# Two heads at a time in attention and retention, with a fixed matmul order, in a two-layer float32 backbone

## The chip, the cores and the metric

The kernel runs on one core of a Trainium2 chip. The metric is the device time of one execution in microseconds, from runs on that core. Its engines are TensorE (PE; PEld is its weight load), VectorE (DVE), ScalarE (ACT), GpSimd (POOL) and SyncE (SP), which here only issues DMAs. Matmuls write to PSUM, which has eight banks of 512 float32 columns on 128 partitions.

## What is computed

Two layers over 256 latent tokens and 256 context tokens of width 1024, all in float32. Each layer: a modulated RMSNorm, one input projection into three parallel groups (neighbourhood attention with 8 heads of 64, a convolution module of 256 channels and 31 taps, and bidirectional retention with 4 heads of key width 32 and value width 64), an output projection, a gated residual, then a feed-forward part: dense in layer 0, eight experts with two per token in layer 1. Layer 1 needs no context output.

```
px = ux @ w_in                       # 3072 columns: q, k, v | conv | ret q, k, v, two gates
s  = concat(q k_window + bias, q k_ctx);  p = softmax(s);  o = p v        # 8 heads of 64
y  = conv(a * sigmoid(g), 31 taps) + b;  silu(layernorm(y))
o_n = ((q_n k_n^T) * decay) v_n + (q_n * q_dec) S;   forward and backward # 4 heads, 32 x 64
y_ret = silu(g_f) * norm(o_f) + silu(g_b) * norm(o_b)
h  = h + g1 * (concat(y_na, y_conv, y_ret) @ w_out)
h  = h + g2 * (dense SwiGLU, or sum over the top 2 of 8 experts of p_e * SwiGLU_e)
```

The modulation vectors (shifts, scales, gates) are `silu(c) @ w_mod + b_mod`, 6 x 1024 for each layer.

## The kernel before

Activations are held transposed (channels on partitions, 512 tokens as columns, context first). A float32 product of full precision is made of three matmuls on a high and a low part (`three`, lines 178 to 182): `split` (lines 136 to 146) makes the high part `wh` of a weight with a ScalarE cast (line 143) and the low part `wl` with a VectorE subtraction (line 145). Plain float32 matmuls (scores, products with V, transposes) stand without the split and show as two records each in the trace.

The stages follow each other in the program: `begin` (modulation of the first norm and the convolution's projection), the mixer of layer 0, its output projection, the dense feed-forward, the mixer of layer 1, its output projection with the router, the experts.

In the mixer, `projT` and `projK` take one 1 MB chunk of `w_in` each, in halves q, and accumulate into two PSUM tiles `mm`. A string of letters gives the order in which the steps are written (`ORDER`): for layer 0 convolution (c), retention's q, k, v (r), gates (g), the first half of attention's q, k, v (p), heads 0 and 1 (0), retention's state (S) and its latent block (B), the second half (q), the switch (m) after which every attention or retention step also issues one chunk of the remaining modulation (`self.st`), convolution taps (t), heads 2 and 3 (1), retention's context block (b) and the rest. That is the order of the text. What each engine executes is decided by a scheduler, which moves instructions of all engines by its own estimate of when they are ready; only the experts have a fixed order (`manual_schedule` for PE, DVE and ACT).

Attention (`attn_lat`, from line 550) takes one head after the other: for each of two query tiles the score (line 562) into a `dn` tile, bias and row minimum on VectorE (565), the exponential (566), the reciprocal (567), the scaling (568), four transposes (571), a ScalarE copy (572), and after both tiles four products with V (575) on the 64 columns of the head in a `po` tile. `attn_ctx` (lines 578 to 604) does the same for the context. Retention (`ret_block`, from line 691) makes its decay table `Dm` anew for each head and block (612, 613), the scores on 32 rows (707), four VectorE products, and four matmuls per head on 64 columns (717 to 720); then squares, row sums (725), a power on GpSimd (728), a copy (730), transposes (733) and the gating.

A chunk of modulation (`mod_chunk`) is a 1 MB load into a `raw` tile and four matmuls on 32 columns each (line 229); 16 such chunks are made in the attention of layer 0. The `raw` pool has two buffers, which the weights of the mixer of layer 0 use as well.

In the experts, each pair of experts has its tokens gathered (`gather_x`): four steps, one per block of another expert, each for two of the eight channel tiles (the halves r). A half is four matmuls (1075) into half of one `tp` tile, a ScalarE copy with bias (1078) and a VectorE difference (1079).

PSUM: `mm` 3 banks, `dn` 2, `tp` 2, `po` 1, for the whole program.

## Time and profile before

| | |
|---|---|
| median of 3 runs | 1965.64 us (1965.2 to 1968.17) |
| profiled execution | 1965.71 us, span 1963.9 us |
| TensorE busy | 1870.9 us, 95% |
| VectorE busy | 1493.4 us, 76% |
| ScalarE busy | 1051.4 us, 54% |
| HBM read | 479.24 MB, mean 245 GB/s |

Stages by the time axis of the trace, from the span's start: `begin` to 63.84, projections of layer 0 to 142.48, its attention and retention (with the later projections) to 309.16, output projection to 356, feed-forward to 742, projections of layer 1 from 756 to 817.56, its attention and retention to 913.41, output projection and router to 957, experts to the end. A row of the timeline has start, length, engine, line, operation, tiles, shapes and the number of records merged; what stands in brackets is the idle time before it and what ended it. Records of matmuls on TensorE overlap by their modelled ends, so that a row's length is a little more than its distance to the next.

### The profile page before, as it was taken

How to read it: one execution, taken by the hardware profiler on the slowest of the kernel's cores; microseconds unless marked ns; L12 is line 12 of the kernel's file. 1: busy time of each engine (PE TensorE's matmuls, PEld its weight loads, DVE VectorE, ACT ScalarE, POOL GpSimd, SP SyncE). 2: the span in 40 equal slices, each digit the busy share in tenths (PEclk: the TensorE clock that was granted, in tenths of full speed). 3: DMA queues.
4: the chain of work that ended last, by engine and by line, in shares of the span. 5: the costliest groups of instructions: out<-in, count | busy, mean ns of one | idle time of the engine just before them, and what ended most of it. 6: DMA issues, size and time to landing. Idle time of an engine off the chain costs nothing.

```text
span 1963.9 us, 24506 instructions
## 1 busy us (share of the span) xinstructions
PE 1870.9 (95%) x9198; PEld 1474.9 (75%) x9198; DVE 1493.4 (76%) x2006; ACT 1051.4 (54%) x1371; POOL 108.0 (6%) x99
## 2 busy tenths in 40 slices
PE   5999999999999999999899999999999999999996
PEld 2886648878878789876777777887777877778774
DVE  4875354786545448846699988999899898999997
ACT  3323333332222234335588667677777777767774
POOL 2100011111111011010000000000000000000000
PEclk9999999999999999999899999999999999999998
DMA  8320355465444213315599988999999999999991
GB/s 306 110 90 30 118 209 197 169 235 193 170 156 167 86 43 129 119 53 215 193 388 359 343 333 314 365 360 344 360 354 358 354 351 352 354 359 364 345 402 68
DMA packets 71806, 481.97 MB, mean 245 GB/s; under 512 B 8320, under 2 KB 12544, under 8 KB 14464
## 3 DMA queue, kind: packets, MB, share of 16 engines
q1 hardware_dynamic: 71680, 480.32, 65.4%
q8 instruction: 76, 1.25, 0.3%
q14 instruction: 50, 0.41, 0.1%
HBM read 479.24 MB, written 1.05 MB: 245 GB/s over the span
## 4 chain that ended last, share of the span: by engine, by line
issue 53%; PE 42%; DVE 2%; POOL 1%; ACT 1%; DMA 0%; POOLq 0%; SPq 0%; DVEq 0%; ACTq 0%
PE mm L181 9%; PE mm L180 9%; PE mm L182 9%; PE dn L180 2%; PE dn L182 2%; PE dn L181 2%; PE po L575 1%; PE dn L562 1%; PE mm L229 1%; PE tp L571 1%; PE dn L707 1%; DVE wl L145 1%; POOL rms L728 1%; PE dn L586 0%; PE tp L725 0%
## 5 line engine op out<-in xcount | busy, mean ns | idle before, releaser
L145 DVE TENSOR_TENSOR wl<-rawx,wh 128x1024 fp32r<-128x1024 f32 x496 | 581.8, 1220 | 61.1 <-ACT wh L143 60.1
L143 ACT CAST wh<-rawx 128x1024 fp32r<-128x1024 f32 x496 | 490.2, 1050 | 162.9 <-PE mm L181 92.6
L180 PE MATMUL mm<-wh,xh 128*128 128x512 f32 x896 | 361.6, 404 | 4.0
L182 PE MATMUL mm<-wh,xl 128*128 128x512 f32 x896 | 354.6, 396 | 0.0
L181 PE MATMUL mm<-wl,xh 128*128 128x512 f32 x896 | 354.0, 395 | 0.0
L143 ACT CAST wh<-raw 128x1024 fp32r<-128x1024 f32 x220 | 222.3, 1051 | 202.6 <-PE mm L181 107.2
L145 DVE TENSOR_TENSOR wl<-raw,wh 128x1024 fp32r<-128x1024 f32 x220 | 262.6, 1222 | 51.9 <-ACT wh L143 50.8
L180 PE MATMUL mm<-uh,wh 128*128 128x512 f32 (+1 forms) x664 | 244.5, 371 | 5.2 <-ACT uh L418 4.2
L181 PE MATMUL mm<-ul,wh 128*128 128x512 f32 (+1 forms) x664 | 244.9, 371 | 0.9 <-DVE ul L419 0.4
L182 PE MATMUL mm<-uh,wl 128*128 128x512 f32 (+1 forms) x664 | 243.9, 369 | 0.0
L180 PEld LDWEIGHTS mm<-wh,xh 128*128 128x128 f32 x896 | 168.8, 188 | 49.5 <-ACT wh L143 12.2
L182 PEld LDWEIGHTS mm<-wh,xl 128*128 128x128 f32 x896 | 168.6, 188 | 40.4
L181 PEld LDWEIGHTS mm<-wl,xh 128*128 128x128 f32 x896 | 169.1, 189 | 34.8
L1139 PE MATMUL dn<-wh,hx 128*128 128x512 f32 x448 | 178.2, 398 | 7.5 <-DVE hx L1124 7.5
L1140 PE MATMUL dn<-wl,hx 128*128 128x512 f32 x448 | 177.3, 396 | 0.0
L180 PEld LDWEIGHTS mm<-uh,wh 128*128 128x128 f32 x664 | 125.2, 190 | 34.0 <-ACT uh L418 5.6
L181 PEld LDWEIGHTS mm<-ul,wh 128*128 128x128 f32 x664 | 125.7, 190 | 25.8 <-POOL ul L419 1.9
L182 PEld LDWEIGHTS mm<-uh,wl 128*128 128x128 f32 x664 | 125.9, 190 | 22.0 <-issue 1.1
L1121 ACT CAST hx<-tp 128x512 fp32r<-128x512 f32 x56 | 33.0, 589 | 140.5 <-PE tp L1114 140.5
L1139 PEld LDWEIGHTS dn<-wh,hx 128*128 128x128 f32 x448 | 84.4, 188 | 30.7 <-DVE hx L1124 11.4
L1140 PEld LDWEIGHTS dn<-wl,hx 128*128 128x128 f32 x448 | 84.2, 188 | 20.6
L145 DVE TENSOR_TENSOR wl<-hT,wh 128x1024 fp32r<-128x1024 f32 x70 | 83.3, 1218 | 4.3 <-ACT wh L143 4.3
(294 smaller groups left out, 2617.7 us busy)
## 6 DMA issues: line engine op xcount, KB each, us to landing
rawx<-w_moe SPq DMA_DIRECT2D x148, 1024.0 KB, 6.7
rawx<-w_moed SPq DMA_DIRECT2D x72, 1024.0 KB, 6.7
raw<-w_moe SPq DMA_DIRECT2D x54, 1024.0 KB, 6.7
raw<-w_mod SPq DMA_DIRECT2D x29, 1024.0 KB, 4.8
rawx<-w_mod SPq DMA_DIRECT2D x19, 1024.0 KB, 5.2
raw<-w_moed SPq DMA_DIRECT2D x19, 1024.0 KB, 6.3
hT<-w_moed SPq DMA_DIRECT2D x18, 1024.0 KB, 6.7
hT<-w_moe SPq DMA_DIRECT2D x17, 1024.0 KB, 6.9
```

The costliest lines, as they stand in the source:

```text
L143: nc.scalar.copy(h, r)
L145: nc.vector.tensor_tensor(l, r, h.bitcast(F32), OP.subtract)
L180: mm(ps, ah, bh, start=first, stop=False)
L181: mm(ps, ah, bl, start=False, stop=False)
L182: mm(ps, al, bh, start=False, stop=last)
L229: nc.tensor.matmul(ps[32 * j:32 * j + 32, :], self.cT[:, k, :], w[:, j, :], start=start, stop=stop)
L562: nc.tensor.matmul(sc, self.qT[r0:r0 + 64, hp, q0 + qt * P:q0 + (qt + 1) * P], self.kT[r0:r0 + 64, hp, :], start=True, stop=True)
L571: nc.tensor.transpose(tp[:, kt * P:(kt + 1) * P], p[:, kt * P:(kt + 1) * P], self.ident)
L575: nc.tensor.matmul(po[r0:r0 + 64, 0:256], self.vt[:, kt, h * 64:h * 64 + 64], pt[:, kt, :], start=kt == 0, stop=kt == 3)
L1121: nc.scalar.copy(hx[:, 0], t3)
L1139: mm(pd[n], hh[:, k], wh[:, 0, c], start=b == 0 and k == 0, stop=False)
L1140: mm(pd[n], hh[:, k], wl[:, 0, c], start=False, stop=b == NB - 1 and k == 3)
```

## The change

- Attention: `lat_unit` and `ctx_unit` take both heads of a pair at once. The two scores go into the two banks of one tile (`pair`), next to each other in the order; the products with V alternate between the two heads.
- Retention: the scores of two heads alternate into two `mm` tiles; the products alternate between two heads in one `md` tile. Decay tables are made once for each layer and head (`decays`) in the gate step.
- `attention` and `retention` are generators, a unit's score ahead of the previous unit's transposes and the unit before's output. `weave` mixes them by their numbers of steps, and `core` runs the mix under `manual_schedule` for TensorE alone: 25 and 20 steps in layer 0, 17 and 12 in layer 1.
- Convolution taps, three at a time, and the modulation chunks of layer 0 become a background (`self.bg`), of which `projT` and `projK` take one step ahead of each group of twelve or 24 matmuls. All projections now stand before `core`.
- `core` takes bias, transposed p and retention's products from three `uu` tiles.
- PSUM has two layouts (`banks`): in the mixers a pair of 2 banks, `mm` 2, `md` 1, `tp` 2, `po` 1; in feed-forward and experts as before.
- `gather_x`: the matmuls of both halves first, then the copies of both; in the steps among the experts into `po` instead of `tp`.

The core of the diff:

```diff
+    def pair(self):
+        t = self.psx.tile([P, 2, 512], F32, name="mmp", tag="mmp")
+        return [t[:, 0], t[:, 1]]
...
-        pss = [self.mm() for _ in range(2)]
+        pss = [self.mm(), self.mm()]
...
                     a, e = cut or (los[m], NTOK)
+                    next(self.bg, None)
...
+        for hh in heads:
+            r = slice(64 * hh, 64 * hh + 64)
+            nc.tensor.matmul(scs[hh], self.qT[r, hp, q0 + qt * P:q0 + (qt + 1) * P], self.kT[r, hp, :], start=True, stop=True)
...
+        def out():
+            po = self.po()
             for kt in range(4):
+                for hh in heads:
+                    h = 2 * hp + hh
+                    nc.tensor.matmul(po[64 * hh:64 * hh + 64, 0:256], self.vt[:, kt, h * 64:h * 64 + 64], pts[hh][:, kt, :], start=kt == 0, stop=kt == 3)
...
+    def attention(self, l, yt):
+        turn = out = None
+        for hp in range(4):
+            pts = []
+            for qt in (0, 1, 2)[:3 if l == 0 else 2]:
+                unit = self.lat_unit(l, hp, qt, yt, pts) if qt < 2 else self.ctx_unit(hp, yt)
+                yield
+                if out:
+                    out()
+                if turn:
+                    turn[0]()
+                    yield
+                out = turn[1] if turn else None
+                turn = unit
...
+            for n, (lo, hi, t) in enumerate(((0, 256, 0), (128, 256, 1), (256, 512, 1), (256, 384, 0))):
+                for pr in range(2):
+                    h = 2 * c + pr
+                    nc.tensor.matmul(od[64 * pr:64 * pr + 64, lo:hi], self.rv[:, g * 2 + t, h * 64:h * 64 + 64], parts[pr][n],
+                                     start=state is None and n == 0, stop=n == 3)
...
+        with self.tc.manual_schedule(engines={mybir.EngineType.PE}):
+            n = (25, 20) if l == 0 else (17, 12)
+            for _ in self.weave((n[0], self.attention(l, yt)), (n[1], self.retention(l, yt))):
+                pass
...
-    ORDER = ("crgp0SBqmt1b23M", "kcrgp0SBqt123")
+    ORDER = ("cxrgpqtA", "kcxrgpqtA")
...
+                    "x": lambda: setattr(self, "bg", self.weave((21, V["taps"]), (17, V["mods"])) if l == 0 else V["taps"]),
...
-            ps = self.dn() if first and q % 2 else self.tp()
-            for r in range(2):
-                c = slice(r * 256, r * 256 + 256)
+            ps = (self.dn() if q % 2 else self.tp()) if first else self.po()
+            cs = [slice(r * 256, r * 256 + 256) for r in range(2)]
+            for r, c in enumerate(cs):
                 k = 2 * q + r
                 for j, ut in enumerate((self.uth, self.utl)):
                     for t in range(2):
                         nc.tensor.matmul(ps[:, c], ut[:, t, k * P:(k + 1) * P], Gr[:, t, :], start=j + t == 0, stop=j + t == 2)
+            for r, c in enumerate(cs):
+                k = 2 * q + r
```

TensorE in the attention of layer 0, about its middle, before: a row is line, operation, tiles written and read, shape and count; L229 is modulation, L562 and L586 are scores, L575 products with V, L571 and L598 transposes.

```order
L229 MATMUL mm<-raw,cTp 32x512 x3
L586 MATMUL dn<-kT,qT 128x256 x3
L575 MATMUL po<-pT,vt 64x256 x4
L571 MATMUL tp<-cst,p 128x128 x4
L229 MATMUL mm<-raw,cTp 32x512
```

The same place in the changed kernel, in its fixed order: L572 and L608 are scores, L763 retention's scores, L636 products with V of the context, L588 transposes, L781 retention's products, L788 its row sums and L797 the transposes after them.

```order
L797 MATMUL mm<-cst,rmb 128x128 x4
L572 MATMUL mmp<-kT,qT 128x512 x2
L763 MATMUL mm<-mix 128x256 x4
L636 MATMUL po<-bx,vt 64x256 x4
L588 MATMUL tp<-cst,p 128x128 x8
L608 MATMUL mmp<-kT,qT 128x256 x4
L781 MATMUL md<-rx,rsd 64x256 x2
L781 MATMUL md<-rx,rsd 64x128 x2
```

The single-head groups of four and the modulation between them are gone; scores and products stand in pairs of heads, with eight transposes in a row.

SyncE's issues from the end of `begin` through the projections of layer 0, before: `raw<-w_in` is a projection's weight chunk, `raw<-w_mod` a modulation chunk, `bias<-nab` the attention bias.

```order
L133 DMA raw<-w_in 128x2048 x2
L781 DMA tab<-tab 128x1536
L560 DMA bias_413<-nab 128x256
L560 DMA bias_414<-nab 128x256
L133 DMA raw<-w_in 128x2048 x8
```

The same stretch of the changed kernel:

```order
L148 DMA raw<-w_in 128x2048
L242 DMA raw<-w_mod 128x2048
L663 DMA tab<-tab 128x1536
L568 DMA bias_415<-nab 128x256
L568 DMA bias_416<-nab 128x256
L242 DMA raw<-w_mod 128x2048
L148 DMA raw<-w_in 128x2048
L242 DMA raw<-w_mod 128x2048 x2
```

Between two weight chunks now stand one or two modulation chunks, in the same two buffers; this goes on until the last of the 16.

## Rows read from the trace of the kernel before

**Rows 1.** The page: span, and busy time of each engine.

```profile
span 1963.9 us, 24506 instructions
PE 1870.9 (95%) x9198; PEld 1474.9 (75%) x9198; DVE 1493.4 (76%) x2006; ACT 1051.4 (54%) x1371; POOL 108.0 (6%) x99
```

**Rows 2.** Stages: stretch, length, busy and records by engine, granted clock, DMA.

```profile
core 0: us, PE busy (x) PEld busy (x) DVE busy (x) ACT busy (x) POOL busy (x), PEclk, DMA share, GB/s
...
63.84:142.48 78.64, 78.64 (x433) 67.95 (x431) 67.38 (x96) 19.64 (x24) 0.00 (x0) 1.00 0.27 95
142.48:309.16 166.68, 158.47 (x771) 88.38 (x771) 76.40 (x206) 60.45 (x136) 13.25 (x9) 1.00 0.35 124
...
817.56:913.41 95.85, 90.90 (x474) 60.20 (x473) 51.54 (x133) 39.74 (x84) 7.68 (x9) 1.00 0.21 70
...
956.63:1963.90 1007.27, 963.89 (x4331) 772.26 (x4330) 919.52 (x987) 725.29 (x832) 0.73 (x1) 0.99 0.89 337
```

**Rows 3.** Groups on TensorE, 142.48 to 309.16: count | busy us, mean ns | idle before.

```profile
L229 PE MATMUL mm<-raw,cTp 128*32 128x512 f32 x128 | 28.5, 605 | 0.0
L562 PE MATMUL dn<-kT,qT 64*128 64x512 f32 x32 | 17.4, 634 | 0.0
L575 PE MATMUL po<-pT,vt 128*64 128x256 f32 x64 | 15.5, 385 | 0.0
...
L586 PE MATMUL dn<-kT,qT 64*128 64x256 f32 x32 | 9.4, 415 | 0.0
L707 PE MATMUL dn<-mix 32*128 32x256 f32 x32 | 9.4, 413 | 0.0
...
L603 PE MATMUL po<-pTc,vt 128*64 128x256 f32 x28 | 7.5, 392 | 0.0
...
L717 PE MATMUL po<-af,rsd 128*64 128x256 f32 x16 | 5.1, 403 | 0.3 <-DVE af L710 0.3
...
L718 PE MATMUL po<-af,rsd 128*64 128x128 f32 x16 | 3.2, 279 | 0.0
```

**Rows 4.** The same view of layer 1's attention, 817.56 to 913.41.

```profile
L562 PE MATMUL dn<-kT,qT 64*128 64x512 f32 x32 | 16.2, 634 | 0.5 <-DVE st L565 0.5
L575 PE MATMUL po<-pT,vt 128*64 128x256 f32 x64 | 15.5, 385 | 0.2 <-ACT pT L572 0.2
```

**Rows 5.** Single rows of TensorE's timeline in layer 0's attention: start, length.

```profile
183.57 0.38 PE L719 MATMUL po<-ab,rsd 128*64 128x256 f32 x1
183.58 0.43 PE L717 MATMUL po<-af,rsd 128*64 128x256 f32 x1
...
220.80 1.12 PE L562 MATMUL dn<-kT,qT 64*128 64x512 f32 x2
...
222.34 0.60 PE L571 MATMUL tp<-cst,p 128*128 128x128 f32 x4
...
226.47 1.13 PE L586 MATMUL dn<-kT,qT 64*128 64x256 f32 x6
227.53 1.94 PE L575 MATMUL po<-pT,vt 128*64 128x256 f32 x8
...
276.03 1.06 PE L229 MATMUL mm<-raw,cTp 128*32 128x512 f32 x8
```

**Rows 6.** The page's DMA issues: count, size each, median us to landing.

```profile
raw<-w_mod SPq DMA_DIRECT2D x29, 1024.0 KB, 4.8
```

**Rows 7.** The power on GpSimd (group, layer 0), and a wait behind it (layer 1).

```profile
L728 POOL TENSOR_TENSOR rms<-rms,cst 128x8 f32<-128x8 f32 x4 | 6.8, 1690 | 155.2 <-DVE rms L727 155.2
...
859.80 0.63 PE L733 MATMUL tp<-cst,rmb 128*128 128x128 f32 x4 [1.57 <-DVE rmb L730]
```

**Rows 8.** Waits of the gather: total, times, longest; and one of them.

```profile
PE tp L1075 <- DVE xl L1079: 14.3, 12, 1.6
...
1140.76 0.51 PE L1075 MATMUL tp<-Gr,uth 128*128 128x256 f32 x2 [1.08 <-DVE xl L1079]
```

**Rows 9.** A long idle gap of TensorE, and the stretch with the lower clock after it.

```profile
33.04 0.50 PE L180 MATMUL mm<-uh,wh 128*128 128x512 f32 x1 [4.17 <-ACT uh L418]
...
33.84:37.25 3.41, 3.29 (x8) 2.29 (x9) 2.68 (x5) 2.00 (x3) 1.88 (x2) 0.50 0.57 229
```

More of the change, by code (lines that the diff above doesn't have):

```diff
@@ L288, in mod_sums, with mod_all @@
             yield
-    def mod_all(self, l, groups, hold):
+    def mod_all(self, l, groups):
         for g in groups:
-            yield from self.mod_steps(l, g, hold)
+            yield from self.mod_steps(l, g)
     def mcol(self, l, ct, v):
@@ L452, in projK @@
         uh, ul = u
-        pss = [self.mm() for _ in range(2)]
+        pss = [self.mm(), self.mm()]
         first = [True, True]
@@ L459, in projK @@
                 c = slice((t % 2) * 256, (t % 2) * 256 + 256)
+                if t % 2:
+                    next(self.bg, None)
                 for k in range(4):
@@ L587, in attn_ctx, with ctx_unit @@
+        return turn, out if qt else None
+    def ctx_unit(self, hp, yt):
+        nc = self.nc
+        heads = (0, 1)
+        scs, ps, pts = self.pair(), [], []
+        for qt in range(2):
+            for hh in heads:
+                r = slice(64 * hh, 64 * hh + 64)
+                nc.tensor.matmul(scs[hh][:, qt * 256:qt * 256 + 256], self.qT[r, hp, qt * P:(qt + 1) * P], self.kT[r, hp, 0:256], start=True, stop=True)
+        for hh in heads:
+            sc = scs[hh]
             st = self.sm.tile([P, 6], F32, name="stc", tag="stc", bufs=4)
@@ L601, in attn_ctx, with turn @@
-            self.st()
-            for kt in range(2):
-                nc.tensor.matmul(po[r0:r0 + 64, 0:256], self.vt[:, kt, h * 64:h * 64 + 64], pt[:, kt, :], start=kt == 0, stop=kt == 1)
-        nc.vector.tensor_copy(yt[0][:, hp, 0:256], po[:, 0:256])
-    def decay(self, l, h):
+            ps.append(p)
+        def turn():
+            for hh in heads:
+                tp = self.tp()
+                for kt in range(2):
+                    for qt in range(2):
+                        nc.tensor.transpose(tp[:, kt * 256 + qt * P:kt * 256 + (qt + 1) * P], ps[hh][:, qt * 256 + kt * P:qt * 256 + (kt + 1) * P], self.ident)
+                pt = next(self.turned).rearrange("p (k q) -> p k q", k=2)
+                nc.scalar.copy(pt, tp.rearrange("p (k q) -> p k q", k=2))
+                pts.append(pt)
@@ L607, in decay, with decays @@
+    def decays(self, l):
+        self.nc.sync.dma_start(self.tab, self.A["tab"])
+        self.Dm = self.mx.tile([P, 4, 2, 256], F32, name="Dm")
+        for h in range(4):
+            self.decay(l, h, self.Dm[:, h])
+    def decay(self, l, h, Dm):
         nc = self.nc
-        Dm = self.mx.tile([P, 2, 256], F32, name="Dm", tag="p", bufs=4)
         for d in range(2):
@@ L737, in ret_block, with retention, weave, core @@
             nc.vector.tensor_tensor(yt[1][:, 2 + c, y0:y0 + 256], r[:, 0:256], r[:, 256:512], OP.add)
+            yield
+    def retention(self, l, yt):
+        self.rope()
+        yield
+        yield from self.ret_state(l)
+        yield from self.ret_block(l, 1, yt, True)
+        if l == 0:
+            yield from self.ret_block(l, 0, yt, None)
+    def weave(self, *streams):
+        done = [0] * len(streams)
+        live = list(range(len(streams)))
+        while live:
+            i = min(live, key=lambda i: (done[i] + 0.5) / streams[i][0])
+            done[i] += 1
+            if next(streams[i][1], self) is self:
+                live.remove(i)
+            else:
+                yield
+    def core(self, l, yt):
+        nc = self.nc
+        x = self.u8(name="bx")
+        for i in range(2):
+            nc.gpsimd.memset(x[:, i, 0:256], 0.0)
+        self.bias = cycle(self.bias + [x[:, i] for i in range(2)])
+        y, z = self.u8(name="rx"), self.u8(name="px")
+        self.turned = cycle([x[:, i] for i in (2, 3)])
+        self.pT = [z[:, 2 * i:2 * i + 2].rearrange("p a (k q) -> p (a k) q", k=2) for i in range(2)]
+        self.spare = cycle([y[:, i] for i in range(4)])
+        with self.tc.manual_schedule(engines={mybir.EngineType.PE}):
+            n = (25, 20) if l == 0 else (17, 12)
+            for _ in self.weave((n[0], self.attention(l, yt)), (n[1], self.retention(l, yt))):
+                pass
     MID = 4
     WCYC = 3
+    TAPS = 3
     CUTS = ((0, 256), (256, 512))
-    ORDER = ("crgp0SBqmt1b23M", "kcrgp0SBqt123")
+    ORDER = ("cxrgpqtA", "kcxrgpqtA")
     def mixer(self, l, u=None, pss=None):
@@ L1213, in run @@
             tps, hx = [], []
-            at = {0: [silu], 2: jobs[0:1], 4: jobs[1:2], 6: [lambda: next(gather, None)] if b else []}
+            at = [(0, silu), *zip((2, 4), jobs), (6, lambda: b and next(gather, None))]
             pu = self.wblock(X[e], at)
@@ L1271, in build @@
             return
+        self.banks(False)
         self.ffn()
+        self.banks(True)
         self.make_A(1, 0)
```

190 lines of the change are left out of this document (92 added, 98 removed).

## The prediction

> **What bounds the kernel now.** I read the page first, then a table by stage, then the matmul groups of one stage, then single rows. The page [rows 1] gives TensorE 95% busy against 76% for VectorE and 54% for ScalarE, so I look for TensorE work and for stretches where it waits. By stage [rows 2]: the projections (63.84 to 142.48 in layer 0) are solid TensorE. The attention stages, where one would expect waiting on softmax, are nearly solid too: 158.47 of 166.68 us busy in layer 0, 90.90 of 95.85 in layer 1, while VectorE does 76.40 and 51.54. The scheduler fills every softmax wait with projection matmuls, modulation chunks and retention. So the mixer is bound by TensorE's own work, and a change pays there only by making that work shorter, not by hiding waits. The experts (956.63 to 1963.90) have TensorE at 963.89 of 1007.27, VectorE at 919.52 and the DMA engines at 0.89: TensorE first, VectorE close behind.
>
> The work can be made shorter because part of it fills half the array. Scores take 64 rows of it (32 for retention), the products with V 64 columns. Alone, a 512-column score of two records takes 1.12 [rows 5], and eight records of 256 columns for one head take 1.94, about 0.234 a record from start to start. But where two heads happen to stand next to each other the records run together: 183.57 and 183.58 start two different heads' matmuls 0.01 apart; six score records at 226.47 are over when the next row starts 1.06 later, where six at 0.234 would take 1.40; and a modulation chunk (four matmuls on four column strips) takes 1.06 for eight records, as long as one matmul alone.
>
> **The change, part by part.** The profiled execution took 1965.71, 0.07 from the median 1965.64; its span is 1963.9, and I sum against 1965.7.
>
> *Pairs in layer 0.* The rows of [rows 3] that become pairs are L562, L575, L586, L603, L707, L717 and L718, with L719 and L720 of the same shapes and counts as the last two: 17.4 + 15.5 + 9.4 + 7.5 + 9.4 + 2 x (5.1 + 3.2) = 75.8 busy, half of it 37.9. Busy times lap over their neighbours; counted by pace it is 192 records of 256 columns at 0.234, 32 of 512 at 0.53 and 32 of 128 at 0.11, together 65.5, half 32.7. Some already run paired, so I take **-30** (20 to 37).
>
> *Pairs in layer 1.* L562 and L575 again, 16.2 + 15.5 [rows 4], and half of layer 0's retention, 13.0: half is 22, by pace 20. I take **-18.5** (12 to 22).
>
> *Modulation.* L229 has 28.5 busy for 16 chunks [rows 3]; unsplit they cost 16 x 1.06 = 17.0 [rows 5]. Before, the scheduler breaks chunks into one matmul and three, which costs two turns instead of one. In the new order all but one of the 16 stand as four together. **-10**.
>
> *Waits that vanish.* The idle of the two attention stages, 8.2 + 4.9 [rows 2]: **-13**.
>
> *Waits that come.* The woven core has a fixed TensorE order and none of the 512-column projections as filler. I walked the printed order of layer 0 by hand with the durations of [rows 5]. Work alone: scores 8 x 1.12 + 4 x 1.06, turns 24 x 0.60, products 4 x 1.94 + 4 x 1.0, retention about 5 a block (x4) and 4 for rope and state, some 64 us. The head of the core waits for rope and the first softmax, about 6; three of the four retention blocks have only one short group between the row sums (L725 before) and the transposes that need them, while the power on GpSimd alone takes 1.69 [rows 7]. Before, this same wait showed as 1.57 on TensorE; I count 1.5 x 3. The tail, the last context heads, about 3. **+14** in layer 0 (core about 77 us). Layer 1 has two blocks and no context heads, 9 + 16 x 0.60 + 8 + 10 + 4 = 41 of work: **+11** (core about 52).
>
> *The ring of two buffers.* In layer 0 the modulation loads now share two `raw` buffers with w_in, and each load waits in SyncE's order behind the one before. A load lands 4.8 after its issue [rows 6]; a chunk of projections takes 78.64 / 7 = 11.2. In total 26 loads x 4.8 / 2 = 62 us against some 135: hidden on average. But a weight load that can start only when the modulation chunk in the middle of its predecessor is consumed has about 5.6 + 1 us until it is needed, less 4.8, and then has to be converted. Below: 0, as before the change. Above: some 1.7 on each of ten chunks, 17. The order leaves the matmuls just about enough time, so I take **+5**. Conversions and bias loads queue behind a late load, but both are earlier than needed. The convolution taps are on VectorE in the projections before as well (67.38 of 78.64 busy), so their move costs nothing; if they delay evacuations it is in the next term.
>
> *Two accumulation buffers instead of three.* Every projection now waits for the evacuation of the previous one with the same buffer; with 512 columns 2.8 us lie between, with 256 columns 1.4. I take **+3** for layer 1 and **+3** for both output projections (0 to 12 together).
>
> *Decay tables* are made once per layer, on ScalarE and VectorE inside the projections: nothing on TensorE.
>
> *Gather.* Before, the second half's matmuls wait until VectorE has read the first half from the same PSUM tile: 12 waits, 14.3 us [rows 8], for example 1.08 before 1140.76. The new order issues both halves first, into `po`, which is free at that point of the block. The experts are TensorE-bound, so up to 14.3 comes back; VectorE's own waits for the copies shrink with it, but it is 91% busy. I take **-13** (0 to 14).
>
> Sum: -30 - 18.5 - 10 - 13 + 14 + 11 + 5 + 6 - 13 = -48.5; 1965.7 - 48.5 = **1917**.
>
> **The rivals.** (a) *The softmax chain becomes the bound.* With TensorE's part halved, a unit of two heads still needs its two reductions, exponentials and scalings before it can be turned. VectorE's share of the layer 0 core is about 57 of its 76.40 (the rest is splits, convolution and halved decay work) beside 64 for TensorE. If units don't overlap, 12 units and 8 units at about 8 us give 96 + 64 = 160 instead of 77 + 52: +31, **1948**. For it: both loads are near each other, and orders on VectorE are fixed where it waits for GpSimd. Against it: one unit's turn and the previous unit's output lie between a score and its turn. The Trainium skill's page TensorEngine Tiling (Array Packing), section Performance Considerations (PSUM Bottleneck), speaks for this rival: it says that tiling speeds up TensorE but not the evacuation of PSUM, which may become the bottleneck. By that rule this rival's time would hold; no row here shows a core without filler.
>
> (b) *The gather's gain stays hidden* behind VectorE's 91%: **1930**.
>
> (c) *The pairs don't run side by side* when issued in this order, so that the change doesn't do what it says: 30 + 18.5 come back, **1965.5**, no change. Against it stand the rows that show overlap between heads.
>
> (d) *The clock falls in the core; slower.* After 4.17 us without a matmul the granted clock stood at 0.50, 1.2 instead of 2.4 GHz, from 33.84 to 37.25 [rows 9]; in the attention stages, with hardly an idle gap, it is 1.00 [rows 2]. The woven cores have more gaps. The price is that the core's 64 + 41 = 105 us of matmuls take twice as long: if all of it runs at the lower level, 1917 + 105 = **2022**. It decides the sign once more than 48.5 / 105 = 46% of this work runs slow. Against it: my gaps are 1 to 2 us, and the 1.57 before 859.80 [rows 7] left layer 1's attention at 1.00 [rows 2]. The Trainium skill's page TensorE: Matmul & The Clock Gate, section "A second HAM failure mode: psum-queue depth-cycling", says that short idle times between groups of matmuls can be enough for the clock to go back and forth. By that rule this rival would happen; the trace before agrees only for the long gap.
>
> **How the numbers follow.** Forecast as summed 0.68; (a) 0.15; (b) 0.08; (c) 0.03; (d) 0.06. The forecast's own bounds are about 1898 (all pairs at their halves, no ring stall) to 1937. The range goes from 1893 to 1953, which takes in (a) and (b) and leaves out (c), (d) and little more. A measurement of this kernel can tell about 0.2%, 4 us. Faster: 0.68 + 0.15 + 0.08 = 0.91; same 0.03; slower 0.06.
>
> **What would show it.** In the changed profile: four score records of 512 columns in about 1.1 us and eight products in about 1; layer 0's first output projection near 281 instead of 309, its core near 77 us, layer 1's near 52; modulation rows of four matmuls, 1.06 each, between projection rows without waits on DMA; no wait of the gather's second half, and experts shorter by about 13. Wrong would be: projections of layer 0 beyond 145 us (the ring), cores over 95 and 70 us with TensorE waiting for VectorE (rival a), records in single file (c), a granted clock under 1.00 in the cores (d), or a gather whose saving turns up as waits on converted weights (b).

## The result, and the profile of the changed kernel

The changed kernel takes 1918.36 us (median of 4 runs), the kernel before 1966.51 beside it: ratio 0.976, interval 0.974 to 0.978. The prediction was 1917.0. The profiled execution took 1918.13, its span is 1916.3, against 1965.71 and 1963.9 before. First the page, for [rows 1]:

```profile
span 1916.3 us, 24478 instructions
PE 1821.2 (95%) x9198; PEld 1452.0 (76%) x9198; DVE 1490.4 (78%) x1998; ACT 1042.7 (54%) x1363; POOL 108.4 (6%) x103
```

The stages, for [rows 2]: stretch, length, busy time and count of TensorE, its weight loads, VectorE, ScalarE and GpSimd, granted clock, DMA share, GB/s. The rows are layer 0's projections, its core, its output projection; layer 1's projections and core; routing and experts.

```profile
core 0: us, PE busy (x) PEld busy (x) DVE busy (x) ACT busy (x) POOL busy (x), PEclk, DMA share, GB/s
62.55:201.86 139.31, 137.97 (x785) 103.15 (x783) 83.65 (x123) 31.73 (x43) 1.91 (x3) 1.00 0.56 198
201.86:280.15 78.29, 63.61 (x425) 39.54 (x424) 57.00 (x172) 40.78 (x105) 10.56 (x8) 0.96 0.16 53
280.15:327.66 47.51, 46.75 (x382) 46.00 (x383) 19.69 (x26) 13.60 (x23) 11.63 (x13) 1.00 0.33 122
...
715.00:825.81 110.81, 106.63 (x789) 101.06 (x788) 80.87 (x160) 43.73 (x72) 2.41 (x5) 0.98 0.30 102
825.81:874.43 48.62, 42.10 (x258) 25.30 (x258) 36.28 (x106) 25.08 (x60) 6.86 (x8) 0.93 0.23 74
...
911.64:1916.30 1004.66, 970.33 (x4356) 774.34 (x4356) 923.70 (x1012) 726.16 (x836) 0.96 (x2) 0.99 0.89 339
```

The two mixers have changed their shape: projections are solid, and the cores (attention and retention together), nearly solid before, now have waits: 78.29 - 63.61 = 14.7 us in layer 0. From the first projection to the output projection layer 0 takes 217.6 instead of 245.3.

The same TensorE groups as [rows 3], in layer 0's core, with the modulation group of the projections as last row (line, tiles, count | busy us, mean ns | idle before):

```profile
L572 PE MATMUL mmp<-kT,qT 64*128 64x512 f32 x32 | 9.7, 687 | 5.6 <-ACT p L615 3.5 <-DVE st L576 2.0
L596 PE MATMUL po<-px,vt 128*64 128x256 f32 x64 | 9.0, 429 | 0.0
L781 PE MATMUL md<-rx,rsd 128*64 128x256 f32 (+1 forms) x64 | 6.8, 335 | 0.1
L636 PE MATMUL po<-bx,vt 128*64 128x256 f32 x32 | 5.0, 393 | 0.1
L763 PE MATMUL mm<-mix 32*128 32x256 f32 x32 | 4.6, 400 | 0.0
L608 PE MATMUL mmp<-kT,qT 64*128 64x256 f32 x32 | 4.5, 402 | 0.0
...
L244 PE MATMUL md<-raw,cTp 128*32 128x512 f32 x128 | 18.1, 605 | 0.5 <-DMA raw<-w_mod 0.5
```

Counts are as before (four of L603's records lay just behind the stretch of [rows 3]), and a record is about as long as before, but busy time is half: the attention and retention groups 75.8 before, 9.7 + 9.0 + 6.8 + 5.0 + 4.6 + 4.5 = 39.6 now; modulation 28.5 before, 18.1 now. What TensorE waits for in that core (line waited for: us in total, times, longest):

```profile
PE mm L797 <- DVE rmb L793: 4.6, 3, 2.1
PE mmp L572 <- ACT p L615: 3.5, 3, 1.6
PE mmp L572 <- DVE st L576: 2.0, 1, 2.0
PE tp L742 <- ACT px L589: 1.2, 1, 1.2
PE mm L788 <- ACT rsq L784: 0.9, 2, 0.6
PE tp L588 <- ACT px L589: 0.7, 1, 0.7
```

And this is new: the granted clock in three stretches of the cores, in the columns of the stages (the 13th word is the clock):

```profile
206.41:209.82 3.41, 2.98 (x10) 1.14 (x6) 3.41 (x10) 0.97 (x3) 0.00 (x0) 0.50 0.29 81
271.26:274.67 3.41, 3.41 (x16) 2.05 (x18) 3.28 (x9) 1.02 (x4) 0.00 (x0) 0.50 1.00 423
831.04:837.87 6.83, 6.15 (x19) 3.32 (x18) 5.88 (x20) 3.44 (x9) 0.00 (x0) 0.50 0.20 57
```

In them TensorE runs at 1.2 instead of 2.4 GHz (two scores of one pair take 2.08 at 834.60, 1.13 elsewhere), so I count half of its busy time there as lost, an estimate: (2.98 + 3.41) / 2 = 3.2 us in layer 0, 6.15 / 2 = 3.1 in layer 1. The first and the third follow a wait of 2.04 in the head of the core, the second the longest of the waits before L797, 2.1. The timeline shows the first of these waits (start, length, engine, line, [idle before <- what ended it]):

```profile
203.59 1.23 DVE L160 TENSOR_TENSOR wl<-raw,wh 128x1024 fp32r<-128x1024 f32 x1 [3.08 <-ACT wh L158]
204.73 0.68 DVE L576 CUSTOM_DVE_ANT_0 p<-mmp,bias 128x512 f32<-128x512 f32 x1
...
205.34 0.69 DVE L576 CUSTOM_DVE_ANT_0 p<-mmp,bias 128x512 f32<-128x512 f32 x1
...
206.09 1.82 PE L572 MATMUL mmp<-kT,qT 64*128 64x512 f32 x4 [2.04 <-DVE st L576]
```

The scores were there about 203.0, but VectorE had the split of an output weight ahead of the first maximum in its order, and that split itself waited for ScalarE. The second score, 1.13 elsewhere, takes 1.82.

### The profile page after: what moved, and what is told of

Same layout as the page of the kernel before. It is cut to its first block, busy times and chain, and to the rows that moved or that the text cites. A ratio compares the mean times of both kernels' runs of the same rounds, so it can differ in the third digit from the quotient of the medians.

```text
span 1916.3 us, 24478 instructions
## 1 busy us (share of the span) xinstructions
PE 1821.2 (95%) x9198; PEld 1452.0 (76%) x9198; DVE 1490.4 (78%) x1998; ACT 1042.7 (54%) x1363; POOL 108.4 (6%) x103
## 4 chain that ended last, share of the span: by engine, by line
issue 53%; PE 27%; DVE 3%; ACT 1%; POOL 1%; POOLq 0%; DVEq 0%; ACTq 0%
PE mm L195 6%; PE mm L196 6%; PE mm L197 6%; PE dn L195 2%; PE dn L197 2%; PE dn L196 2%; DVE wl L160 1%; DVE mix L511 1%; PE po L596 1%; PE mmp L572 0%; PE tp L588 0%; ACT wh L158 0%; ACT uh L437 0%; POOL ms L402 0%; PE tp L289 0%
## 5 line engine op out<-in xcount | busy, mean ns | idle before, releaser
L160 DVE TENSOR_TENSOR wl<-rawx,wh 128x1024 fp32r<-128x1024 f32 x496 | 581.5, 1220 | 66.1 <-ACT wh L158 64.9
L197 PE MATMUL mm<-uh,wl 128*128 128x512 f32 (+1 forms) x656 | 239.5, 367 | 0.0
L195 PEld LDWEIGHTS mm<-wh,xh 128*128 128x128 f32 x896 | 168.7, 188 | 49.5 <-ACT wh L158 7.8
L1233 PEld LDWEIGHTS dn<-wh,hx 128*128 128x128 f32 x448 | 84.3, 188 | 33.7 <-DVE hx L1218 15.5
```

The lines of the kernel that those rows point to most:

```text
L160: nc.vector.tensor_tensor(l, r, h.bitcast(F32), OP.subtract)
L195: mm(ps, ah, bh, start=first, stop=False)
L197: mm(ps, al, bh, start=False, stop=last)
L1233: mm(pd[n], hh[:, k], wh[:, 0, c], start=b == 0 and k == 0, stop=False)
```

## Experiments

Every experiment starts from the changed kernel. Since most concern the cores, here is one table of their profiles: length from the first score to the first low half of the output projection (`mm<-yl`); TensorE's busy time in it; how much of that is loss at half clock (half of the busy time in the stretches at 0.50, as above); and the rest of the length, its waits. Work at full clock (busy less loss), loss and waits add up to the length by the way they are counted. All in us.

| kernel | total | ratio to before (interval) | layer 0's core: length, busy, loss, waits | layer 1's core: length, busy, loss, waits |
|---|---|---|---|---|
| changed | 1918.4 | 0.9762 (0.9741-0.9783) | 78.3, 63.6, 3.2, 14.7 | 45.6, 39.1, 3.1, 6.5 |
| gather_halves | 1930.0 | 0.9823 (0.9810-0.9837) | 79.4, 64.9, 4.3, 14.5 | 44.5, 37.6, 1.5, 6.9 |
| heads_apart | 1927.6 | 0.9815 (0.9800-0.9830) | 83.6, 70.1, 4.4, 13.5 | 46.7, 40.9, 1.4, 5.9 |
| heads_far | 1933.2 | 0.9838 (0.9823-0.9853) | 82.3, 72.6, 3.2, 9.7 | 49.5, 43.9, 3.1, 5.6 |
| core_scheduled | 1919.0 | 0.9759 (0.9745-0.9772) | 78.5, 69.5, 6.5, 9.0 | 47.0, 43.1, 3.4, 3.9 |
| state_early | 1917.5 | 0.9757 (0.9744-0.9771) | 80.6, 65.4, 7.9, 15.2 | 38.3, 33.9, 1.7, 4.5 |
| head_filled | 1919.5 | 0.9763 (0.9750-0.9777) | 78.9, 65.3, 2.9, 13.6 | 44.0, 38.3, 0, 5.8 |
| rms_later | 1927.7 | 0.9800 (0.9787-0.9813) | 86.5, 71.9, 9.3, 14.6 | 47.0, 40.1, 3.4, 6.9 |
| ctx_copied | 1918.7 | 0.9760 (0.9746-0.9773) | 80.5, 68.7, 9.1, 11.8 | 44.0, 36.5, 0, 7.5 |
| l1_early_tail | 1913.7 | 0.9732 (0.9719-0.9745) | 79.7, 65.2, 5.1, 14.5 | 37.0, 32.5, 0, 4.5 |
| no_scaling | - | - | 72.6, 59.5, 0, 13.1 | 44.9, 38.9, 3.1, 6.0 |
| filled | 1908.1 | 0.9704 (0.9690-0.9718) | 74.1, 67.7, 0, 6.4 | 37.0, 32.5, 0, 4.5 |
| filled_only | 1918.8 | 0.9753 (0.9739-0.9768) | 75.6, 68.4, 0, 7.2 | 44.0, 39.5, 0, 4.5 |

A caution on totals: the opening, which no edit touches, ended (first projection) at 31.8 us in the changed kernel's profile and between 32.7 and 35.4 in the others, so totals can't tell apart 2 or 3 us; stage lengths can.

A caution on the loss too: it differs between profiles of the same instructions. Layer 1's core is not edited in gather_halves and ctx_copied, and yet its loss is 3.1 in the changed kernel, 1.5 and 0 in these two, its length 45.6, 44.5 and 44.0. So with one profile for each kernel, 3 us of loss or 1.6 of length there are not yet the work of an edit. They also show that only half of the loss reached the length: of 3.1 us of it 1.6 did, and with less loss the waits were longer (6.5, 6.9, 7.5). Layer 0's core, unedited in gather_halves, lost 3.2 and 4.3 and took 78.3 and 79.4.

**gather_halves: the gather undone.**

```
-            ps = (self.dn() if q % 2 else self.tp()) if first else self.po()
+            ps = self.dn() if first and q % 2 else self.tp()
...
                         nc.tensor.matmul(ps[:, c], ut[:, t, k * P:(k + 1) * P], Gr[:, t, :], start=j + t == 0, stop=j + t == 2)
-            for r, c in enumerate(cs):
-                k = 2 * q + r
                 b = self.mcol(1, 24 + k, 0)
```

> The changed kernel with one part undone: each half of a gather step is scaled by ScalarE and VectorE before the second half's matmuls are issued, in the PSUM tile used before. Theory (the 12 waits of 1.1 to 1.25 us were TensorE's own path): they come back, 10 to 13 us slower than the changed kernel, 1928 to 1931. Rival (the gain is a side effect of something else in the experts, or is hidden behind VectorE): within 4 us of 1918. Third case, neither: about 1923, half of the waits was covered by converted weights coming late.

Measured 1930.02, 11.7 more. The stretch from the routing on, 1004.66 in the changed kernel, is 9.7 longer:

```profile
913.54:1927.90 1014.36, 969.34 (x4356) 777.57 (x4356) 924.27 (x1012) 726.95 (x836) 0.97 (x2) 0.99 0.89 336
```

The gather's matmuls in the experts, of the changed kernel and then of this one (count, ns, first and last start; below it, idle time of TensorE before them, or who waited for them):

```profile
L1167 PE MATMUL po<-Gr,uth x48: 277/281/287, 1081.1 to 1631.4; 128*128 128x256 f32 x48
its engine sat idle before it (us, times) until:
who waited for it (us, times):
  ACT xh L1172: 22.3, 12
```

```profile
L1167 PE MATMUL tp<-Gr,uth x48: 277/281/392, 1083.3 to 1644.5; 128*128 128x256 f32 x48
its engine sat idle before it (us, times) until:
  DVE xl L1171: 14.3, 12
```

The 12 waits of [rows 8] are back with their 14.3 us, and of these 9.7 lie in the length of the experts; the other 2 us of the total are in stretches that the edit does not touch (1.4 of them in the opening). The theory holds, but VectorE, 92% busy, took a part of the gain back. Without the 12 waits TensorE waits longer for the experts' SwiGLU products (`sg`) on VectorE; this wait in the changed kernel, then in this one (total, times, longest):

```profile
PE tp L1208 <- DVE sg L1311: 4.4, 15, 0.9
...
PE tp L1206 <- DVE sg L1309: 1.9, 3, 0.9
```

**heads_apart, heads_far: without pairs.** In the first the heads of a unit follow each other (the first diff, and the same exchange in the context units and the retention); in the second `out(hh)` issues one head's products with V, and other work lies between the two.

```
-            for kt in range(4):
-                for hh in heads:
+            for hh in heads:
+                for kt in range(4):
```
```
+                if out:
+                    out(0)
                 unit = self.lat_unit(l, hp, qt, yt, pts) if qt < 2 else self.ctx_unit(hp, yt)
                 yield
                 if out:
-                    out()
+                    out(1)
```

> The changed kernel with the same units, buffers and weave, but within a unit the products with V, the context scores and all retention scores and products are issued for one head and then for the other; only the pair of 512-column scores stays side by side. By the changed kernel's rows single file adds 1.85 to each of 8 L596 groups, 0.75 to each of 4 L608, 0.8 to each of 4 L636, 0.75 to each of 6 L763 and 1.3 to each of 6 L781: 33 us of TensorE work. Theory (running side by side is what makes the cores short): the cores' busy time rises by about 33, the waits of 21 us shrink by some 8, so 20 to 30 us slower than the changed kernel, 1938 to 1948. Rival (the fixed order and the weave carry the gain, pairs do not matter): within 6 us of 1918.

> The changed kernel with the products with V taken apart for good: head 0's are issued ahead of the next unit's scores, head 1's behind them, so that the two heads of a unit have 4 or more other matmuls between them (in the run before, where the heads only followed each other, half of the records still ran together: 16 records of L596 took 2.86 against 1.90 side by side and 3.74 at the pace of one). Retention and scores stay as in the changed kernel. Theory (side by side is worth TensorE time, and about 0.8 of such time ends up in the total, as 9.4 of 11.9 did there): 8 L596 groups at +1.85 and 4 L636 at +0.8 make 18 us of work, 10 to 18 us slower than the changed kernel, 1928 to 1936. Rival (the cores are bound by the chains of VectorE and ScalarE, so this work falls into waits of 15 and 6.5 us): within 5 us of 1918.

heads_apart cost 9.2, not 20 to 30: my price was wrong, since issuing one head after the other does not put them in single file. At full clock only L596 and L781 of the six groups grew, and by half of what single file would cost; 8 records of two heads (L608, L636) run at full clock as fast as interleaved. The two groups in layer 0's core of heads_apart, then the products of heads_far, for 9.0 and 5.0 above:

```profile
L596 PE MATMUL po<-px,vt 128*64 128x256 f32 x64 | 11.4, 385 | 0.0
...
L781 PE MATMUL md<-rx,rsd 128*64 128x256 f32 (+1 forms) x64 | 8.9, 332 | 0.0
```
```profile
L597 PE MATMUL po<-px,vt 128*64 128x256 f32 x64 | 17.0, 413 | 0.4 <-ACT px L589 0.4
...
L640 PE MATMUL po<-bx,vt 128*64 128x256 f32 x32 | 7.6, 391 | 0.6 <-DVE yt L600 0.6
```

With work between them the products take 17.0 (one group of eight ran at half clock, 3.54 instead of 1.94), so they are as long again as the 15.5 before the change, and the total rises by 14.9, as expected. In the profile it is 13.8, of which 11.2 lie in the two cores and in the stretch behind the second, where its last products stand. So the products with V owe their gain to standing side by side. For the scores and the retention no run took the heads as far apart; that pairs carry their gain is read from the groups above, which halved at equal counts. Not all of the added time arrives in layer 0: there busy time at full clock rose by (72.6 - 3.2) - (63.6 - 3.2) = 9.0, waits fell by 5.0, and the core grew by 4.0.

**core_scheduled: the order not fixed.**

```
-        with self.tc.manual_schedule(engines={mybir.EngineType.PE}):
+        if True:
```

> The changed kernel with TensorE's order in the two cores left to the scheduler instead of fixed by the weave. In the printed order the pairs mostly stay, retention scores move up into the head of the core, and some groups are cut in two. Theory (the waits of the core come from its chains; the fixed order is worth little by itself): within 5 us of 1918, with the head's waits of 2.04, 0.68 and 1.23 partly filled. Rival (the fixed order is what keeps the pairs and the waits small): 8 to 20 us slower, 1926 to 1938.

Measured 1919.0, the same. The scheduler's order waits 5.7 less in layer 0 (9.0), but cuts pairs (2.5 us more work at full clock) and has 3.3 more of loss at half clock. The fixed order by itself brings nothing that the total shows.

**state_early: less work in the head.**

```
     def retention(self, l, yt):
-        self.rope()
-        yield
-        yield from self.ret_state(l)
...
-    ORDER = ("cxrgpqtA", "kcxrgpqtA")
+    ORDER = ("cxrgSpqtA", "kcxrgSpqtA")
...
+                    "S": lambda: self.early_state(l),
```

> The changed kernel with rope and retention state of each layer moved from the head of the core into the projections, before the last two query and key projections, so that the core's weave starts with retention scores. Theory (the head's waits, 2.04 + 0.68 + 1.23 in layer 0 and 2.04 + 0.68 + 0.35 in layer 1, and the stretch at half clock that follows each are due to too little TensorE work there): waits of the head shrink to about 2 per layer, the clock stays at 1.00 there, core about 70 and 43; 6 to 10 us faster than the changed kernel, 1908 to 1912. Rival (the softmax chain of VectorE and ScalarE sets the pace of the core; work taken out of it turns into waits): within 3 us of 1918. Rival two (VectorE is full in the projections, the five rope and state operations there delay evacuations): slower than 1921.

Measured 1917.5, the same: the first rival by its number, but not by its mechanism. In layer 1 the core became 7.3 us shorter, the stretch behind it 1.5 longer. In layer 0 2.9 us less work (65.4 - 7.9 against 63.6 - 3.2) met equal waits and 4.7 us more loss at half clock, in stretches after waits in the middle of the core; the moved work made the projections before it 2.3 longer.

**head_filled, rms_later, ctx_copied: one wait each.** In this order:

```
         self.rope()
+        ps = self.tp()
+        for i in range(2):
+            self.nc.tensor.matmul(ps, self.ident, self.kT[:, i, :], start=True, stop=True)
```
```
             yield
+            yield
             rb = self.mm()
...
-            n = (25, 20) if l == 0 else (17, 12)
+            n = (25, 24) if l == 0 else (17, 14)
```
```
-            nc.vector.tensor_reduce(st[:, 0:2], sc.rearrange("p (q k) -> p q k", q=2), AX.X, OP.max, negate=True)
...
-                nc.scalar.activation(p[:, qt * 256:qt * 256 + 256], sc[:, qt * 256:qt * 256 + 256], AF.Exp, bias=st[:, qt:qt + 1], accum_out=st[:, 2 + qt:3 + qt])
+                nc.vector.tensor_tensor_reduce(p[:, qt * 256:qt * 256 + 256], sc[:, qt * 256:qt * 256 + 256], self.zeros, -1.0, 3e38, OP.add, OP.min, st[:, qt:qt + 1])
+            for qt in range(2):
+                nc.scalar.activation(p[:, qt * 256:qt * 256 + 256], p[:, qt * 256:qt * 256 + 256], AF.Exp, bias=st[:, qt:qt + 1], scale=-1.0, accum_out=st[:, 2 + qt:3 + qt])
```

> The changed kernel with two matmuls of 512 columns (2.1 us, result unused) in each core's head, behind the rope matmuls, where TensorE waits 2.04 us for the first maximum; nothing waits for them. Theory (that wait is what lets the granted clock fall to 0.50 from 206.4 to 209.8 and from 831.0 to 837.8, and rows there take twice as long, by their rows about 1.5 and 3.2 us): the wait is filled, the clock stays at 1.00 in both heads, the cores are 1 to 1.5 and 2 to 3 us shorter, 1913 to 1916. Rival (the clock falls later instead or the rows' extra time lies in waits for VectorE and ScalarE): cores as long as before within 0.5 us, 1916 to 1920.

> The changed kernel with one step more of attention between the row sums of a retention block (L788) and the transposes of their power (L797). Theory (each wait of the core is its own link of VectorE and GpSimd, and goes when more TensorE work lies in it): the waits of 1.37, 1.10 and 2.12 before L797 in layer 0 and of 1.73 in layer 1 go, and the stretch at half clock from 271.3 with them: 5 to 7 us faster than the changed kernel, 1911 to 1913. Rival (the chain through VectorE and ScalarE sets the pace): the waits move to the softmax of the context heads (L572 behind L615), within 2.5 us of 1918.

> The changed kernel with the context heads' scores read once by VectorE, which writes them to SBUF with their maximum, so that ScalarE's exponentials no longer hold the PSUM pair. Theory (TensorE waits 1.65, 1.61 and 0.27 before L572 because four exponentials of 0.47 + 0.20 have to leave the only pair of score banks): these waits shrink to under 0.5 each, 3 to 4 us less in layer 0 and nothing in layer 1, 1914 to 1915. Rival (VectorE, 57 of 78 us busy and with more to do now, is late next): within 1.5 us of 1918 or slower.

head_filled: in layer 1 the clock stayed at 1.00 and the core is 1.6 shorter, but so it is in ctx_copied, where nothing in that core is filled (44.0 in both): the fill does not show as the reason. In layer 0 the wait of 2.04 became 0.32, the next ones 0.68 and 1.70, and the clock fell at 212.9 instead of 206.4; nothing gained, and nothing in the total. rms_later: my theory fell. The three waits before L797 became one of 1.70, but the score behind the context heads' exponentials now waits 3.33, all waits together stay at 14.6, and the loss at half clock is 9.3; 9.3 slower. (Its busy time at full clock is also 2.2 higher: 1.5 of it are the retention's products L781, 8.3 instead of 6.8, whose groups are now cut by waits for their inputs.) ctx_copied: the waits behind L615 went as expected, 14.7 to 11.8 in all, and the core is longer. Its core, the stretches of it at half clock, and its layer 1's core, which the edit leaves alone:

```profile
204.05:284.51 80.46, 68.71 (x425) 42.92 (x424) 58.42 (x196) 40.91 (x105) 10.60 (x8) 0.87 0.15 51
208.70:218.90 10.20, 8.75 (x28) 5.38 (x26) 7.14 (x25) 3.16 (x9) 0.00 (x0) 0.50 0.19 52
256.50:263.30 6.80, 5.94 (x24) 2.41 (x20) 4.24 (x12) 1.52 (x4) 1.63 (x1) 0.50 0.00 0
277.00:280.40 3.40, 3.40 (x18) 1.74 (x15) 1.88 (x4) 0.26 (x1) 0.00 (x0) 0.50 0.65 275
...
829.93:873.94 44.01, 36.52 (x240) 22.43 (x240) 34.64 (x104) 23.93 (x58) 6.06 (x6) 1.00 0.18 53
```

(8.75 + 5.94 + 3.40) / 2 = 9.05 us are lost here, 5.9 more than in the changed kernel, for 2.9 fewer of waits. The unedited core lost 3.2 and 4.3 in two profiles; this is more, though from one profile. It formed the next theory: what one wait gives, the clock can take back elsewhere.

**no_scaling, l1_early_tail: is it the chain of VectorE?** The first leaves out the scaling by the softmax's sums, in the context units too, and so computes other values; only its cores are compared.

```
-            nc.vector.reciprocal(st[:, 2:3], st[:, 1:2])
-            nc.vector.tensor_scalar(p, p, st[:, 2:3], None, OP.mult)
```
```
+        if l == 0:
+            self.rope()
+            yield
+            yield from self.ret_state(l)
...
+    ORDER = ("cxrgpqtA", "kcxrgSpqtA")
...
-                (nc.vector if k % 2 else nc.gpsimd).tensor_tensor(b, c, a.bitcast(F32), OP.subtract)
+                nc.vector.tensor_tensor(b, c, a.bitcast(F32), OP.subtract)
```

> The changed kernel without the reciprocals and scalings of the softmax (it leaves the exponentials undivided): per unit two reciprocals of 0.16 and 0.96 to 1.2 of scalings on VectorE, some 15 us of its 57 in layer 0's core and 9 of 36 in layer 1's. TensorE's work is the same. Values change, and with them what the routing and the experts do, so only the two cores are compared. Theory (layer 0's core of 78 us is set by the chain through VectorE and ScalarE, layer 1's mostly by TensorE): layer 0's core 5 to 12 us shorter, 66 to 73, layer 1's less than 3 us shorter. Rival (both are set by TensorE's work in its fixed order): both within 2 us of 78.3 and 45.6 (from the first score to the first low half of the output projection).

> The changed kernel with two edits at different places. One: rope and retention state move into the projections in layer 1 alone (moved in both layers, they made the stretch from the first score to the experts 5.2 us shorter in layer 1, but layer 0's core 2.3 longer and the projections before it 2.3). Two: the low halves of the heads' outputs are all made by VectorE, where GpSimd made every second one (it holds up the power of the last retention block by 0.9 before 271.16 and the output projection by 1.46 + 0.47 at 280.15). Theory (layer 1's core is bound by TensorE's own work and the waits of its head, layer 0's by its chain of VectorE and ScalarE): 5 us less in layer 1, 1.5 to 3 us less at the end of layer 0's core, 1909 to 1913. Rival (what was won in layer 1 was chance of one profile): 1915 to 1918, from the second edit alone or from neither.

no_scaling's cores:

```profile
205.67:278.28 72.61, 59.48 (x425) 37.92 (x424) 43.59 (x116) 41.00 (x105) 10.80 (x8) 1.00 0.17 57
825.00:869.88 44.88, 38.93 (x241) 23.90 (x240) 26.51 (x73) 24.01 (x58) 6.08 (x6) 0.92 0.17 52
```

The number came (72.6, 5.7 shorter) and yet the theory did not: VectorE has 13.4 us less to do, but the waits went only from 14.7 to 13.1. More than half of the 5.7 is the clock, which stood at 1.00 here (3.2 of loss gone), though the head's wait of 2.04 is still there; it fell 2.2 us behind the core instead, and the output projection is 1.2 longer. So VectorE's load doesn't set the core. That the waits are latencies of single links is argued from this, not shown. l1_early_tail took 1913.7, 4.6 faster than the changed kernel (their intervals just meet): layer 1's early state is a gain, 37.0 instead of 45.6 in that core (89.3 instead of 96.0 from its first score to the experts, of which 1.6 can be the clock alone, as in ctx_copied). At the end of layer 0's core one wait of 1.12 stands for the 1.46 and 0.47; the one of 2.1 before L797 stayed, so GpSimd's other work had not caused it.

**filled, filled_only: the clock kept up.** Matmuls whose results nobody reads stand ahead of the waiting instructions (the diff is from filled, with three of its places). filled also has the edits of l1_early_tail and ctx_copied, and fills layer 0 alone; filled_only has this edit alone, in both layers.

```
+    def fill(self, n):
+        if n:
+            ps = self.po()
+            for i in range(n):
+                self.nc.tensor.matmul(ps[:, 0:256], self.ident, self.kT[:, 0, 0:256], start=True, stop=True)
...
             self.rope()
+            self.fill(4)
...
+            self.fill({(1, 0): 2, (0, 0): 1, (0, 1): 4}.get((g, c), 0) if l == 0 else 0)
             rb = self.mm()
```

> Three edits together. Layer 1's early state and VectorE's low halves as in the run before (1913.7). The context heads' scores copied out of PSUM by VectorE, which alone shortened layer 0's waits from 14.7 to 11.8 us and still made the core 80.5 instead of 78.3 long, with the granted clock at 0.50 for 20.4 us of it. And matmuls with unused results (256 columns, 0.53 each, 16 in all) put into layer 0's core just ahead of the instructions that wait there: 4 in the head's wait of 2.04, 1 and 2 in the next two, 2 to 4 ahead of the row sums and transposes of the retention blocks. Theory (the clock ate what the shorter waits gave): TensorE's own work in that core is 60 at full clock and its waits 12, so with the clock at 1.00 the core is 71 to 73 instead of 78 to 80, 1905 to 1908. Rival (the chain of VectorE and ScalarE sets the core's length, so that slow matmuls only fill waits): core 77 to 80 whatever the clock shows, 1911 to 1915. Third case: the clock falls all the same, since the gaps between the filling matmuls remain, and the core is over 77 with over 5 us at 0.50.

> The changed kernel with nothing but filling matmuls (256 columns, 0.53 each, results unused) ahead of the instructions that wait in the two cores: in layer 0 seven in the head, two ahead of each of two scores that wait for the context heads' exponentials, two, one and three ahead of the transposes of three retention blocks; in layer 1 five in the head and two ahead of the first block's transposes. In the changed kernel's profile the clock at 0.50 cost 3.2 us in layer 0's core and 3.1 in layer 1's (half of TensorE's busy time in those stretches). Theory (the cores' length is TensorE's work at full clock, the waits, and that loss): clock at 1.00 in both cores, 78.3 and 45.6 become 75 and 42.5, 1911 to 1913. Rival (slow matmuls only fill waits that are there anyway): the clock at 1.00 and yet cores of 77.5 to 79 and 45 to 46, 1916 to 1920.

The two cores of filled, then of filled_only:

```profile
205.56:279.64 74.08, 67.66 (x458) 44.33 (x457) 58.30 (x199) 40.79 (x105) 6.53 (x4) 1.00 0.17 56
826.63:863.62 36.99, 32.48 (x219) 19.86 (x218) 29.69 (x95) 22.59 (x55) 3.27 (x2) 1.00 0.19 55
```
```profile
204.80:280.41 75.61, 68.39 (x460) 43.96 (x459) 56.90 (x172) 40.99 (x105) 10.56 (x8) 1.00 0.16 54
827.71:871.73 44.02, 39.54 (x255) 24.87 (x254) 34.52 (x104) 24.06 (x58) 6.07 (x6) 1.00 0.18 53
```

In all four the clock is 1.00. filled has 6.4 us less in layer 0's core than ctx_copied and takes 1908.1: the fastest kernel here, 3% under the kernel before, and 5.6 under l1_early_tail, whose interval it does not touch. Against l1_early_tail its layer 0 core has 7.6 us more work, 8.1 less of waits and 5.1 less of loss. filled_only's cores are 2.7 and 1.6 shorter than the changed kernel's. In layer 0 the fill adds 68.4 - 60.4 = 8.0 of work and takes 7.5 of waits away, so what is gained is the loss of 3.2 less 0.5. In layer 1 nothing is shown: its 44.0 are also the length of ctx_copied's unfilled core. Its total, 1918.8, does not show the gain either. The opening of its profile was 3.3 longer, five runs from 1912.8 to 1919.7 can't settle 4 us, and the clock fell 1.6 us behind layer 0's core instead, which made the output projection 1.0 longer:

```profile
281.98:285.39 3.41, 3.29 (x15) 3.29 (x16) 3.41 (x4) 0.93 (x1) 0.06 (x1) 0.50 0.12 14
```

So that the lower level costs core time is shown by the stages, in layer 0 by filled and filled_only; that keeping it away shows in the total is shown only together with the two other edits, in filled.

## Why the prediction was right, term by term

Measured terms are differences of stages: busy time at full clock (loss taken out), waits, loss.

| term | forecast | measured |
|---|---|---|
| layer 0: pairs and modulation | -30 - 10 | 237.1 to 201.6 busy, 3.2 of it loss: -38.7 (modulation -10.4) |
| layer 0: waits gone, waits new, ring | -8.2 + 14 + 5 = +10.8 | 8.2 to 16.0: +7.8 |
| layer 1: pairs | -18.5 | 164.15 to 148.73, 3.1 of it new loss: -18.5 |
| layer 1: waits gone, new, buffers | -4.9 + 11 + 3 = +9.1 | 5.7 to 10.7: +5.0 |
| both output projections | +3 | 47.17 to 47.51 and 35.94 to 37.21: +1.6 |
| clock in the cores | 0 (rival d) | +3.2 + 3.1 = +6.3 |
| routing and experts: gather | -13 | 1014.55 to 1004.66: -9.9 (9.7 when undone) |
| opening, up to the projections | 0 | -1.3 |
| sum | -48.5 | -47.7 |

**What held.** TensorE's own work bounds the mixer, and it shrank by what was forecast, in both layers within 1.5 us. That side by side is the cause is shown by heads_far for the products with V; for the scores and retention it is read from the halved groups. Modulation came out as its single rows said, 18.1 / 16 = 1.13 for a chunk, one turn each; no run undid it alone. The gather's waits were TensorE's own path, as gather_halves shows.

**What was off, and cancelled.** That the total came within 1.4 us is luck: waits came out 7 us below the forecast in the two mixers, against 6.3 of clock that had no term and a gather that gave 3 less. In layer 0 the core's 14.7 were forecast as 14, but the ring of two buffers, priced at 5, has one wait of 0.5 for a modulation load (last row of the groups). In layer 1 the core waits 6.5 instead of 11; its projections wait 4.2, with 1.8 of that behind evacuations of the accumulation buffers (0.9, 0.7 and 0.2), where 3 was forecast, and 1.7 behind the convolution taps, whose move had been priced at nothing. The gather's 13 became 9.9, in the main since the wait before L1208 grew from 1.8 to 4.4. And the clock was priced as all or nothing, 105 us or none, where it took 6.3. The cores came out at 78.3 and, to its last product, 48.6 against 77 and 52. In layer 0 that is 60.4 of work at full clock and 14.7 of waits, where 64 and 14 were forecast, and 3.2 of loss; in layer 1 39.0 and 6.5, where 41 and 11 were forecast, and 3.1 of loss. A right total hid a missing term. The step that failed is the argument against rival (d): that waits of 1 to 2 us leave the clock alone, from one wait of 1.57. Here 2.04 was followed by the lower level, twice, and 2.1 once. The Trainium skill's page TensorE: Matmul & The Clock Gate, section "A second HAM failure mode: psum-queue depth-cycling", which was cited for this rival, agrees with the traces here: short waits between groups were enough. They did not always do it: the same 2.04 left layer 1's core at 1.00 in ctx_copied, and what decides between the two stays open.

**The other rivals.** (a) fell: with a quarter of VectorE's work in the core gone the waits are 13.1 instead of 14.7. (b) fell with gather_halves. (c) fell with the groups' busy times.

## What to carry to other kernels

Work that fills half of the array is cheap to pair: what counted here is that two heads' matmuls stand next to each other in the queue, not the fixed order around them. When work taken out of a core leaves waits behind, read the granted clock of that core, and of the stage behind it, before chasing the waits one by one, and take more than one profile: the loss moved by 3 us between profiles of the same instructions. Cheap matmuls without use, put ahead of waits that stay, kept layer 0's core at full clock here, where removing a wait (ctx_copied) gained nothing.

## What the runs showed of the hardware that was not expected

- The granted clock fell to 0.50 for 3.4 or 6.8 us, in three kernels for over 10, in cores whose longest wait is 1.8 to 3.3 us; yet the same wait of 2.04 left it at 1.00 in layer 1's cores of ctx_copied, l1_early_tail and filled and in layer 0's of no_scaling. With the longest wait at 1.2 (layer 0's core of filled) it stayed at 1.00, as it did before the change with 1.57.
- The same instructions in layer 1's core lost 3.1, 1.5 and 0 us at half clock in three profiles, and took 45.6, 44.5 and 44.0: half of the loss reached the length, the rest took the place of waits.
- Two heads' products issued one head after the other, 8 records each, overlap by half (2.86 us for 16 records, 1.90 interleaved, about 3.8 with work between); 4 and 4 records take the same as interleaved (1.13).
